# A hybrid decoder layer on one core: the last adaLN split is read wholly in the down projection, and the sums of the tokens' quadrants run on VectorE over more steps

## The chip, the cores and the metric

The kernel runs on one core of one Trainium2 chip. The metric is the device time of one launch in microseconds (us). Engines are named as in the profile: PE is TensorE, DVE is VectorE, ACT is ScalarE, POOL is GpSimd, SP is SyncE, which here only issues DMAs. Each engine takes its own instructions in the order in which they were written.

## The reference, cut to what matters

One decoder layer over 512 tokens of width 2048, all in float32:

```python
mod = jax.nn.silu(c) @ w_ada[l] + b_ada[l]
sh_a, sc_a, gt_a, sh_f, sc_f, gt_f = [m[:, None, :] for m in jnp.split(mod, 6, axis=-1)]
h = rmsnorm(x, g_pre_attn[l]) * (1.0 + sc_a) + sh_a
proj = h @ w_in[l]                     # q, k, v of 8 dilated and 8 differential heads
...
x = x + gt_a * rmsnorm(mix @ w_out[l], g_post_attn[l])
h = rmsnorm(x, g_pre_ffn[l]) * (1.0 + sc_f) + sh_f
f = (jax.nn.silu(h @ w_gate[l]) * (h @ w_up[l])) @ w_down[l]      # D_FF = 5632
x = x + gt_f * rmsnorm(f, g_post_ffn[l])
```

`w_ada` has six splits of 2048x2048, 16 MB each. The last of them gives `gt_f`, which is used only on the output of the down projection.

## The kernel before

**Steps.** All weights pass through one list of 544 steps. A step takes one weight tile of 128x1024 (512 KB), splits it into a high and a low part and multiplies three times (high by high, low by high, high by low), which gives float32 accuracy. The names in the profile: `w_raw` is the tile as it was loaded, `w_hi` its high part (a copy on ACT, L1530), `w_lo` the rest (a subtraction on DVE, L1539); the matmuls stand on L282 to L284. The list has these stages:

- steps 0 to 79: input projections, with attention mixed in;
- W0 + 0 to 63 (W0 = step 80): output projection, 12 matmuls a step. The tokens are done in two halves: the first half's result comes at W0 + 32, and from there its residual, norm (`u`, `x`, `wss`; L1132 to L1156) and transposes into the FFN's input (`h2_tr`, L1178 to L1196) run beside the second half;
- F0 + 0 to 31 (F0 = step 144): gate and up columns of the first of 11 column groups, 12 matmuls a step. In F0 + 0 to 15 the second half's residual, norm and transposes run;
- F1 + 0 to 279 (F1 = step 176): the other ten groups in a Strassen-like form with seven products. Four of these read sums of the tokens' quadrants, the tiles `e`;
- D0 + 0 to 87 (D0 = step 456): down projection, 24 matmuls a step, four column groups of 22 steps.

**Look-ahead.** In step i the kernel makes `w_hi` and `w_lo` of step i + 2 (`do_hi`, `do_lo`). There are three buffers each for `w_hi` and `w_lo`, and a ring of four buffers for `w_raw`; SP issues the next load when a buffer has been used (`pump_loads`).

**adaLN reads.** Four of the six splits (array `in_adar`, 32 tiles of 512 KB each) are read through the same ring of four, as extra items behind a step (`aux[i]`). DVE turns each tile into one column by a multiply with a running sum (L228; `ada_dot`). A planner decides ahead of the run behind which steps they go, with an estimate of when DVE and the DMAs have room. The order is split n = 2, 0, 1, 3; what is left of n = 3 after the output projection goes behind steps D0 + 2 and on. When all of n = 3 is there, three small DVE operations, a transpose on PE and two DMAs through DRAM (`ada_row`) make the row `gtg` of gains, which `d_evac` multiplies to the down projection's result.

**Quadrant sums.** For each of eight chunks j: `e_load` reads the chunk from DRAM (SP), `e_sums` makes four sums of 128x256 on POOL (L1233 to L1236), and `e_split` makes the high part `e` on ACT (L1247) and the low part on DVE (L1248). They stand at F0 + 16 + 2j, + 17 + 2j and + 19 + 2j. The buffers for them are the tiles `stage` and `stageb`.

The order in one step, from the loop that issues all (the quoted lines are not adjacent):

```python
for f in start_ev[i]: f()
s["mm"](*hl[i], 0)                     # first half of the matmuls
do_hi(i + LA)                          # ACT: w_hi of step i + 2
s["mm"](*hl.pop(i), 1)
for f in post_ev[i]: f()
do_lo(i + LA)                          # DVE: w_lo of step i + 2, SP: next loads
for j, (src, f) in enumerate(aux[i]): ...   # DVE: adaLN products, SP: next loads
for f in post_end[i]: f()
```

Of the kernel before, what the change touches and what calls it, by code (L numbers as in the profile page):

```python
# [24 lines left out]
M_ADA = -0.05  # L25
# [9 lines left out]
def body(tc, t):  # L35
# [5 lines left out]
    with ctx:  # L41
# [986 lines left out]
        for i, c in dve_late.items():  # L1028
            dve_cost[i] += c
        todo = [(hn, k, h, qbs) for hn, (k, h) in enumerate(order)  # L1030
                for qbs in (((0,), (1,), (2,), (3,)) if k == "B" else ((0, 1), (2,), (3,)))]
        ada_todo = [(n, ch, hf) for n in (2, 0, 1, 3) for ch in range(16) for hf in range(2)]
        need = defaultdict(int)
# [17 lines left out]
        for i in range(W0 + 60):  # L1051
# [23 lines left out]
            t_dma = max(t_dma, t_pe) + 1.45 * (1 + len(aux[i]))  # L1075
            while ada_todo and (ada_todo[0][0] == 3 or i < W0 + 46) and i >= 1 and t_dve + 1.14 <= t_end + (M_ADA if i < W0 else M_ADAW) and \
                    t_dma + 1.45 <= t_end + M_DMA and len(aux[i]) < NAUX:
                t_dma += 1.45
                n, ch, hf = ada_todo.pop(0)
                aux[i].append((adar[n, ch, hf], ada_use(n, ch, hf)))  # L1080
                t_dve += 1.14
                aux_last = (i, i - W0, n, ch)
                if n < 2:
                    if ch == 15 and hf:
                        post_end[i].append(lambda n=n: ada_cols(n))
                elif n == 2 and ch == 15 and hf:
# [9 lines left out]
        assert not todo and not rq and not rows_todo, (len(todo), len(rq))  # L1096
        assert len(ada_todo) <= 16 and all(a[0] == 3 for a in ada_todo), ada_todo


        start_ev[W0 + 62].append(lambda: [act.dma_start(silud[:, 1024 * h:1024 * h + 1024], silu_h[h]) for h in range(2)])  # L1100

# [5 lines left out]
        for i, (n, ch, hf) in enumerate(ada_todo):  # L1107
            aux[D0 + 2 + i].append((adar[n, ch, hf], ada_use(n, ch, hf)))
        row = ada_row(3, 7)
        post_late[D0 + 18].append(row[0])  # L1110
        mid_ev[D0 + 19].insert(0, row[1])
        start_ev[D0 + 20].append(row[2])

# [104 lines left out]
        def v3(p, a):  # L1218
            return p[1].rearrange("p (a c) -> p a c", a=a)
# [10 lines left out]
        def e_sums(j):  # L1230
            h, e = v3(esum[j], 4), stage.get()
            o = v3(e, 4)
            pool.tensor_tensor(o[:, 0, :], h[:, 2, :], h[:, 3, :], op=OP.subtract)  # L1233
            pool.tensor_tensor(o[:, 1, :], o[:, 0, :], h[:, 0, :], op=OP.subtract)
            pool.tensor_tensor(o[:, 2, :], h[:, 0, :], h[:, 2, :], op=OP.subtract)
            pool.tensor_tensor(o[:, 3, :], h[:, 1, :], o[:, 1, :], op=OP.add)  # L1236
            stage.add(esum[j])
            esum[j] = e

        def e_split(j):  # L1240
            if ("E", 0, 0) not in SA:
                for lo, tags in enumerate((LR[4:], ("P2", "P5", "P0", "P3"))):
                    for m in range(4):
                        SA["E", lo, m] = U(tags[m], [128, 2, 4, 256], R, name=f"e{lo}{m}")
            o = v3(esum[j], 4)
            hi, lo = SA["E", 0, j // 2][:, j % 2], SA["E", 1, j // 2][:, j % 2]
            act.activation(hi, o, AF.Copy)  # L1247
            dve.tensor_tensor(lo, o, hi.bitcast(F), op=OP.subtract)  # L1248
            stage.add(esum.pop(j))
# [71 lines left out]
        def stage_alloc(n):  # L1321
# [275 lines left out]
        for i in range(NSTEP):  # L1597
# [158 lines left out]
```

## Time and profile before

| | us |
|---|---|
| median of 3 runs | 2279.52 |
| lowest and highest run | 2278.01, 2283.3 |
| the profiled execution, its own time | 2278.92 |
| its span in the trace | 2277.1 |
| PE busy in the span | 2222.8 (98%) |
| DVE busy | 1594.9 (70%) |
| ACT busy | 1032.8 (45%) |
| POOL busy | 74.2 (3%) |

The share of busy time says that PE sets the time; the 54 us in which it is idle are few, so they have to be looked for stage by stage. A matmul's end is modelled: each is shown 0.39 us long while the next starts 0.23 us later, so idle time of PE is a little more than the gaps that the trace prints.

### The profile page before, as it was taken

The page shows a single profiled execution, that of the slowest core. Times are in us where ns is not written, and L with a number is a line of the kernel's source. Part 1 is how long each engine was busy: PE and PEld are TensorE (multiplying, and loading weights), DVE is VectorE, ACT ScalarE, POOL GpSimd, SP SyncE. Part 2 cuts the span into 40 slices and gives each one's busy share as a digit, 9 for nine tenths or more (in the row PEclk, how much of TensorE's full clock was granted, in tenths as well). Part 3 has the DMA queues.
Part 4 walks back from the last instruction along what each step waited for, and adds up shares of the span by engine and source line. Part 5 has one row for each costly group of instructions (what it writes and reads, how often), then busy time and mean ns, then how long its engine had stood idle before and what let it go on. Part 6 is the DMA issues. An engine that isn't in the chain of part 4 may idle for free.

```text
span 2277.1 us, 26712 instructions
## 1 busy us (share of the span) xinstructions
PE 2222.8 (98%) x10012; PEld 1808.3 (79%) x10012; DVE 1594.9 (70%) x2201; ACT 1032.8 (45%) x1507; POOL 74.2 (3%) x68
## 2 busy tenths in 40 slices
PE   7999999999999888999999999999999999999998
PEld 6888777778887666778888888888888888888886
DVE  6987877776777786777778777777777644444445
ACT  5443344444435454644454444444444433333432
POOL 0000000000001000150000000000000000000000
PEclk8999999999999999999999999999999999999999
DMA  9796544456778888864224323422432656655564
GB/s 370 296 332 213 157 139 166 145 163 192 222 260 278 300 295 300 276 240 147 94 93 157 130 98 115 157 93 93 157 140 80 252 194 211 195 189 200 189 218 185
DMA packets 124802, 440.11 MB, mean 193 GB/s; under 512 B 13792, under 2 KB 25344, under 8 KB 118272
## 3 DMA queue, kind: packets, MB, share of 16 engines
q1 hardware_dynamic: 105936, 406.14, 51.8%
q10 hardware_dynamic: 18736, 32.27, 4.4%
q8 instruction: 78, 1.28, 0.2%
q14 instruction: 52, 0.43, 0.1%
HBM read 404.25 MB, written 25.18 MB: 189 GB/s over the span
## 4 chain that ended last, share of the span: by engine, by line
PE 83%; DMA 6%; DVE 6%; issue 2%; ACT 2%; POOL 1%; ACTq 0%; SPq 0%; DVEq 0%; POOLq 0%
PE b L283 21%; PE b L284 21%; PE b L282 20%; PE b L277 5%; PE b L279 5%; PE b L278 5%; DMA w_raw<-in_wout 5%; DVE w_lo L1539 2%; PE b L507 2%; PE b L545 1%; ACT w_hi L1530 1%; DVE w_raw L228 1%; PE b L1262 1%; PE b L500 1%; PE b L529 1%
## 5 line engine op out<-in xcount | busy, mean ns | idle before, releaser
L1539 DVE TENSOR_TENSOR w_lo<-w_raw,w_hi 128x1024 fp32r<-128x1024 f32 x264 | 325.6, 1237 | 312.9 <-ACT w_hi L1530 312.5
L1530 ACT ACTIVATE w_hi<-w_raw 128x1024 fp32r<-128x1024 f32 x264 | 278.7, 1057 | 461.6 <-PE b L284 309.2
L283 PE MATMUL b<-w_lo,h 128*128 128x512 f32 x864 | 338.6, 392 | 7.7 <-DVE w_lo L1539 6.2
L282 PE MATMUL b<-w_hi,h 128*128 128x512 f32 x864 | 342.1, 396 | 0.4 <-ACT xT L212 0.4
L284 PE MATMUL b<-w_hi,h 128*128 128x512 f32 x864 | 337.1, 390 | 0.0
L1530 ACT ACTIVATE w_hi<-raw 128x1024 fp32r<-128x1024 f32 x196 | 208.1, 1062 | 268.9 <-PE b L284 244.3
L1539 DVE TENSOR_TENSOR w_lo<-raw,w_hi 128x1024 fp32r<-128x1024 f32 x196 | 240.1, 1229 | 103.1 <-ACT w_hi L1530 102.6
L284 PE MATMUL b<-w_hi,acthl 128*128 128x512 f32 x704 | 274.0, 389 | 0.4 <-DVE acthl L972 0.4
L282 PE MATMUL b<-w_hi,acthl 128*128 128x512 f32 x704 | 274.1, 389 | 0.0
L283 PE MATMUL b<-w_lo,acthl 128*128 128x512 f32 x704 | 273.9, 389 | 0.0
L282 PE MATMUL b<-w_hi,e 128*128 128x512 f32 x640 | 249.7, 390 | 0.0
L283 PE MATMUL b<-w_lo,e 128*128 128x512 f32 x640 | 249.0, 389 | 0.0
L284 PE MATMUL b<-w_hi,e 128*128 128x512 f32 x640 | 249.0, 389 | 0.0
L277 PE MATMUL b<-h,w_hi 128*128 128x512 f32 x512 | 213.4, 417 | 0.0
L278 PE MATMUL b<-h,w_hi 128*128 128x512 f32 x512 | 201.0, 393 | 1.6 <-DVE h L273 1.6
L279 PE MATMUL b<-h,w_lo 128*128 128x512 f32 x512 | 201.6, 394 | 0.0
L283 PEld LDWEIGHTS b<-w_lo,h 128*128 128x128 f32 x864 | 162.3, 188 | 48.1 <-DVE w_lo L1539 15.0
L282 PEld LDWEIGHTS b<-w_hi,h 128*128 128x128 f32 x864 | 162.2, 188 | 37.5 <-issue 3.7
L284 PEld LDWEIGHTS b<-w_hi,h 128*128 128x128 f32 x864 | 162.2, 188 | 33.6
L284 PEld LDWEIGHTS b<-w_hi,acthl 128*128 128x128 f32 x704 | 132.1, 188 | 28.0 <-DVE acthl L972 0.8
L282 PEld LDWEIGHTS b<-w_hi,acthl 128*128 128x128 f32 x704 | 132.1, 188 | 27.8 <-DVE stage L1314 0.2
L283 PEld LDWEIGHTS b<-w_lo,acthl 128*128 128x128 f32 x704 | 132.2, 188 | 27.3
(246 smaller groups left out, 3262.8 us busy)
## 6 DMA issues: line engine op xcount, KB each, us to landing
w_raw<-in_adar SPq DMA_DIRECT2D x128, 512.0 KB, 4.6
raw<-in_wgu SPq DMA_DIRECT2D x109, 512.0 KB, 4.5
w_raw<-in_win SPq DMA_DIRECT2D x107, 512.0 KB, 5.0
actf<-act2d SPq DMA_DIRECT2D x88, 512.0 KB, 4.7
w_raw<-in_wdown SPq DMA_DIRECT2D x88, 512.0 KB, 3.5
w_raw<-in_wout SPq DMA_DIRECT2D x64, 512.0 KB, 4.9
w_lent<-in_wgu SPq DMA_DIRECT2D x51, 512.0 KB, 4.6
ada<-in_ada SPq DMA_DIRECT2D x21, 1024.0 KB, 9.2
```

The costliest lines, as they stand in the source:

```text
L228: dve.scalar_tensor_tensor(w, w, 1.0, silu_h[half], op0=OP.mult, op1=OP.mult, accum_out=dst)
L277: pe.matmul(ps, whi, ahi, start=start, stop=False, **kw)
L278: pe.matmul(ps, whi, alo, start=False, stop=False, **kw)
L279: pe.matmul(ps, wlo, ahi, start=False, stop=stop, **kw)
L282: pe.matmul(ps, ahi, whi, start=start, stop=False, **kw)
L283: pe.matmul(ps, ahi, wlo, start=False, stop=False, **kw)
L284: pe.matmul(ps, alo, whi, start=False, stop=stop, **kw)
L500: pe.matmul(sc[:, r], qk[:, i, qs], qk[:, i + 1, :N], start=True, stop=True)
L507: pe.matmul(sc[:, :N], qk[k, 2 * m, qs], qk[k, 2 * m + 1, :N], start=True, stop=True)
L529: pe.transpose(tr[:, j, :], misc["p"][:, n % 2, 128 * j:128 * j + 128], ident)
L1530: act.activation(hi, raw, AF.Copy)
L1539: dve.tensor_tensor(lo, raw, hi.bitcast(F), op=OP.subtract)
```

## The change

Three things, and small ones that go with them:

1. The planner places the splits n = 2, 0, 1 only. All 32 tiles of n = 3 go behind D0 + 2 to D0 + 33, one a step. The row of gains then comes at D0 + 36 and no longer at D0 + 20, which is after the first column group's evacuation (D0 + 22, 23). So that group is copied out bare, and its gain is multiplied on later (`d_gain`, at D0 + 46, 48, 50, 52). The transpose uses PSUM bank 3 in place of 7. The copy of silu(c) to DRAM, which the late reads need, is issued at W0 + 50 in place of W0 + 62.
2. The quadrant sums run on DVE. They stand at the end of step F0 + 17 + floor(5j/2), the copy on ACT with them, the low part one step later, the load three steps earlier.
3. The transposes of the FFN's input come one step later, in both halves.

```diff
-        ada_todo = [(n, ch, hf) for n in (2, 0, 1, 3) for ch in range(16) for hf in range(2)]
+        ada_todo = [(n, ch, hf) for n in (2, 0, 1) for ch in range(16) for hf in range(2)]
...
-            while ada_todo and (ada_todo[0][0] == 3 or i < W0 + 46) and i >= 1 and t_dve + 1.14 <= t_end + (M_ADA if i < W0 else M_ADAW) and \
+            while ada_todo and i < W0 + 46 and i >= 1 and t_dve + 1.14 <= t_end + (M_ADA if i < W0 else M_ADAW) and \
...
+        ada_todo = [(3, ch, hf) for ch in range(16) for hf in range(2)]
...
-        start_ev[W0 + 62].append(lambda: [act.dma_start(silud[:, 1024 * h:1024 * h + 1024], silu_h[h]) for h in range(2)])
+        start_ev[W0 + 50].append(lambda: [act.dma_start(silud[:, 1024 * h:1024 * h + 1024], silu_h[h]) for h in range(2)])
...
-        row = ada_row(3, 7)
-        post_late[D0 + 18].append(row[0])
-        mid_ev[D0 + 19].insert(0, row[1])
-        start_ev[D0 + 20].append(row[2])
+        row = ada_row(3, 3)
+        post_late[D0 + 34].append(row[0])
+        mid_ev[D0 + 35].insert(0, row[1])
+        start_ev[D0 + 36].append(row[2])
...
-            pool.tensor_tensor(o[:, 0, :], h[:, 2, :], h[:, 3, :], op=OP.subtract)
-            pool.tensor_tensor(o[:, 1, :], o[:, 0, :], h[:, 0, :], op=OP.subtract)
-            pool.tensor_tensor(o[:, 2, :], h[:, 0, :], h[:, 2, :], op=OP.subtract)
-            pool.tensor_tensor(o[:, 3, :], h[:, 1, :], o[:, 1, :], op=OP.add)
+            dve.tensor_tensor(o[:, 0, :], h[:, 2, :], h[:, 3, :], op=OP.subtract)
+            dve.tensor_tensor(o[:, 1, :], o[:, 0, :], h[:, 0, :], op=OP.subtract)
+            dve.tensor_tensor(o[:, 2, :], h[:, 0, :], h[:, 2, :], op=OP.subtract)
+            dve.tensor_tensor(o[:, 3, :], h[:, 1, :], o[:, 1, :], op=OP.add)
...
+            act.activation(SA["E", 0, j // 2][:, j % 2], o, AF.Copy)
+        def e_lo(j):
...
-        post_ev[F0 + 8].append(lambda: stage_alloc(0))
+        post_ev[F0 + 2].append(lambda: stage_alloc(0))
...
-            post_ev[F0 + 16 + 2 * j].append(lambda j=j: e_load(j))
-            post_ev[F0 + 17 + 2 * j].append(lambda j=j: e_sums(j))
-            post_ev[F0 + 19 + 2 * j].append(lambda j=j: e_split(j))
+            at = F0 + 17 + 5 * j // 2
+            start_ev[at - 3].append(lambda j=j: e_load(j))
+            post_end[at].append(lambda j=j: e_sums(j))
+            post_end[at + 1].append(lambda j=j: e_lo(j))
...
-            pe_ev[b1 + 8 + i].append((0, a))
-            post_ev[b1 + 8 + i].append(b)
+            pe_ev[b1 + 9 + i].append((0, a))
+            post_ev[b1 + 9 + i].append(b)
...
-            pe_ev[b1 + 7 + i].append((0, a))
-            post_ev[b1 + 7 + i].append(b)
+            pe_ev[b1 + 8 + i].append((0, a))
+            post_ev[b1 + 8 + i].append(b)
...
-            dve.tensor_tensor(u, ps, GTG[1][:, cg, :], op=OP.mult)
+            if cg == 0:
+                dve.tensor_copy(u, ps)
+            else:
+                dve.tensor_tensor(u, ps, GTG[1][:, cg, :], op=OP.mult)
...
+            if i - D0 in (46, 48, 50, 52):
+                d_gain((i - D0 - 46) // 2)
```

**The loads on SP in the output projection.** In the kernel before, around the load of the tokens `x` for the first half (W0 + 20), an adaLN tile stands behind nearly every second weight tile:

```order
L1515 DMA w_raw<-in_adar 128x1024
L1515 DMA w_raw<-in_wout 128x1024 x2
L1128 DMA x_5898<-in_xtok 128x2048
L1128 DMA x_5900<-in_xtok 128x2048
L1515 DMA w_raw<-in_adar 128x1024
L1515 DMA w_raw<-in_wout 128x1024
L1515 DMA w_raw<-in_adar 128x1024
L1515 DMA w_raw<-in_wout 128x1024 x2
```

In the changed kernel, from the last adaLN tile of the stage to its last weight tile:

```order
L1523 DMA w_raw<-in_adar 128x1024
L1523 DMA w_raw<-in_wout 128x1024 x9
L1129 DMA x_5889<-in_xtok 128x2048
L1129 DMA x_5891<-in_xtok 128x2048
L1523 DMA w_raw<-in_wout 128x1024 x32
L1129 DMA x_6642<-in_xtok 128x2048
L1129 DMA x_6644<-in_xtok 128x2048
L1523 DMA w_raw<-in_wout 128x1024 x6
```

From W0 + 16 on the ring now holds weight tiles alone: 30 adaLN tiles, 15.7 MB, have left this stage for D0 + 2 to D0 + 33.

**DVE and ACT in the second half of the first group (F0 + 17 on).** DVE before, for two chunks; the operation on `e` is the low part of a chunk:

```order
L1539 TENSOR_TENSOR w_lo<-w_raw,w_hi 128x1024 x2
L1248 TENSOR_TENSOR e_7473<-stage_7161,e_7469 128x1024
L1539 TENSOR_TENSOR w_lo<-w_raw,w_hi 128x1024 x2
L1248 TENSOR_TENSOR e_7474<-stage_7392,e_7470 128x1024
L1539 TENSOR_TENSOR w_lo<-w_raw,w_hi 128x1024 x2
```

DVE in the changed kernel, for one chunk and the next one's start:

```order
L1547 TENSOR_TENSOR w_lo<-w_raw,w_hi 128x1024
L1234 TENSOR_TENSOR stage_7304<-stageb 128x256
L1235 TENSOR_TENSOR stage_7304<-stage_7304,stageb 128x256
L1236 TENSOR_TENSOR stage_7304<-stageb 128x256
L1237 TENSOR_TENSOR stage_7304<-stageb,stage_7304 128x256
L1547 TENSOR_TENSOR w_lo<-w_raw,w_hi 128x1024
L1247 TENSOR_TENSOR e_7337<-stage_7304,e_7333 128x1024
L1547 TENSOR_TENSOR w_lo<-w_raw,w_hi 128x1024 x2
L1234 TENSOR_TENSOR stage_6928<-stage_7304 128x256
```

ACT in the changed kernel, around the chunks j = 2 and 3 and the gate of the second half:

```order
L1538 ACTIVATE w_hi<-w_raw 128x1024 x3
L1244 ACTIVATE e_7334<-stage_6928 128x1024
L1538 ACTIVATE w_hi<-w_raw 128x1024 x2
L1244 ACTIVATE e_7334<-stage_7304 128x1024
L1538 ACTIVATE w_hi<-w_raw 128x1024
L1279 ACTIVATE stage_7304<-b_7288 128x512
L1279 ACTIVATE stage_7304<-b_7297 128x512
L1538 ACTIVATE w_hi<-w_raw 128x1024 x2
```

The four sums are now DVE's own, and between them and DVE's next `w_lo` two copies stand on ACT: the chunk's `e`, then the `w_hi` that this `w_lo` reads.

## Rows read from the trace of the kernel before

**Rows 1.** The profile page: busy time by engine, and PE's busy share, in tenths, in 40 slices of 57 us.

```profile
PE 2222.8 (98%) x10012; PEld 1808.3 (79%) x10012; DVE 1594.9 (70%) x2201; ACT 1032.8 (45%) x1507; POOL 74.2 (3%) x68
...
PE   7999999999999888999999999999999999999998
```

**Rows 2.** Busy time by stretch: from and to, length, busy time of PE, PEld, DVE, ACT and POOL (instructions), granted clock, DMA share, GB/s. In order: a stretch of the input projections, W0 + 16 to 63, F0 + 0 to 14, F0 + 15 to F1 + 2, the rest of F1, the first steps of the down projection, a later stretch of it.

```profile
114.00:171.00 57.00, 57.00 (x253) 47.18 (x253) 50.98 (x86) 25.75 (x33) 0.00 (x0) 1.00 0.91 331
...
734.80:903.70 168.90, 146.36 (x609) 113.61 (x608) 124.38 (x175) 77.52 (x117) 3.69 (x4) 0.96 0.86 306
903.70:949.20 45.50, 45.40 (x214) 36.72 (x213) 37.68 (x55) 34.48 (x54) 4.65 (x4) 1.00 0.77 257
949.20:1013.00 63.80, 57.58 (x257) 46.17 (x256) 43.96 (x35) 31.00 (x32) 37.71 (x32) 1.00 0.76 285
1013.00:1784.00 771.00, 769.77 (x3459) 636.09 (x3458) 588.49 (x533) 371.73 (x423) 0.00 (x0) 1.00 0.35 120
1788.00:1804.00 16.00, 16.00 (x77) 13.24 (x76) 11.59 (x12) 8.60 (x12) 0.00 (x0) 1.00 0.99 351
1810.00:1980.00 170.00, 170.00 (x752) 140.65 (x751) 76.12 (x71) 65.17 (x72) 0.00 (x0) 1.00 0.61 204
```

**Rows 3.** Instructions in order of time on PE and, last, the chain of work: the first matmuls of the steps F0 + 0 and F0 + 1 (start, us), then the transposes of two steps that have them (start, us, four of 128x128).

```profile
903.70 0.39 PE L282 MATMUL b<-w_hi,h 128*128 128x512 f32 x1
...
906.42 0.39 PE L282 MATMUL b<-w_hi,h 128*128 128x512 f32 x1
...
926.83 0.44 PE b L1178 x4
930.04 0.44 PE b L1178 x4
```

**Rows 4.** What PE waited for from 734.8 to 903.7 us: us in total, times, the longest.

```profile
PE b L283 <- DVE w_lo L1539: 12.7, 15, 2.5
PE b L282 <- ACT w_hi L1530: 4.5, 3, 3.8
PE b L1178 <- DVE x L1156: 3.7, 1, 3.7
PE b L283 <- DVE wss L1145: 1.5, 1, 1.5
```

**Rows 5.** The same stretch: what the copy `w_hi` waited for (one group on ACT, with its idle time and what ended it), the DMA issues (count, KB each, median us to landing), and the adaLN products on DVE.

```profile
L1530 ACT ACTIVATE w_hi<-w_raw 128x1024 fp32r<-128x1024 f32 x49 | 51.9, 1059 | 85.0 <-DMA w_raw<-in_wout 69.3 <-DVE w_raw L228 6.9 <-PE b L284 5.5
...
L228 DVE SCALAR_TENSOR_TENSOR w_raw<-w_raw,silu_b 128x1024 f32<-128x1024 f32 x16 | 19.5, 1219 | 0.7 <-DMA w_raw<-in_adar 0.7
...
w_raw<-in_wout SPq DMA_DIRECT2D x45, 512.0 KB, 4.9
w_raw<-in_adar SPq DMA_DIRECT2D x29, 512.0 KB, 4.5
x<-in_xtok SPq DMA_DIRECT2D x4, 1024.0 KB, 8.4
```

**Rows 6.** The same stretch: the clock in the three pieces where it was lower, and the chain's step through the slowest weight load (start, us).

```profile
751.10:754.50 3.40, 3.40 (x10) 2.64 (x8) 2.49 (x5) 1.67 (x3) 0.00 (x0) 0.51 0.84 318
819.50:822.80 3.30, 3.10 (x9) 2.61 (x10) 2.59 (x6) 2.41 (x5) 0.00 (x0) 0.50 0.80 245
877.50:884.20 6.70, 4.87 (x11) 3.51 (x12) 5.17 (x6) 3.17 (x3) 0.00 (x0) 0.50 0.86 299
...
867.42 10.22 DMA w_raw<-in_wout
```

**Rows 7.** PE's largest idle time from 949.2 to 1013 us, and what PE waited for in that stretch as a whole.

```profile
994.20 0.50 PE L283 MATMUL b<-w_lo,h 128*128 128x512 f32 x1 [1.93 <-DVE w_lo L1539]
...
PE b L283 <- DVE w_lo L1539: 6.2, 5, 1.9
```

**Rows 8.** ACT and DVE there in order of time: start, us, and in brackets idle time and what ended it.

```profile
957.51 1.06 ACT L1530 ACTIVATE w_hi<-w_raw 128x1024 fp32r<-128x1024 f32 x1 [1.66 <-PE b L284]
...
976.00 1.06 ACT L1247 ACTIVATE e<-stage 128x1024 fp32r<-128x1024 f32 x1 [1.50 <-POOL stage L1236]
976.97 1.04 ACT L1530 ACTIVATE w_hi<-w_raw 128x1024 fp32r<-128x1024 f32 x1
...
990.16 1.06 ACT L1247 ACTIVATE e<-stage 128x1024 fp32r<-128x1024 f32 x1 [3.46 <-POOL stage L1236]
...
958.61 1.23 DVE L1539 TENSOR_TENSOR w_lo<-w_raw,w_hi 128x1024 fp32r<-128x1024 f32 x1 [1.49 <-ACT w_hi L1530]
```

**Rows 9.** Groups by line and shape from 734.8 to 1013 us: the 128x256 operation of two SBUF operands on DVE, one of POOL's sums, products out of PSUM on DVE, and the gate's copy out of PSUM on ACT.

```profile
L1195 DVE TENSOR_TENSOR h<-h2t,h 128x256 fp32r<-128x256 f32 x32 | 13.5, 420 | 2.4 <-ACT h L1194 2.0
...
L1235 POOL TENSOR_TENSOR stage<-stageb 128x256 f32<-128x256 f32 x3 | 5.2, 1718 | 0.0
...
L1281 DVE TENSOR_TENSOR stage<-stage,b 128x512 f32<-128x512 f32 x4 | 2.6, 678 | 1.8 <-ACT stage L1280 1.8
...
L1280 ACT ACTIVATE stage<-b 128x512 f32<-128x512 f32 x4 | 2.2, 592 | 0.0
```

**Rows 10.** DVE in step D0 + 2, the first of the down projection that has an adaLN tile (start, us).

```profile
1800.28 1.23 DVE L1539 TENSOR_TENSOR w_lo<-w_raw,w_hi 128x1024 fp32r<-128x1024 f32 x1 [3.08 <-ACT w_hi L1530]
1801.42 1.22 DVE L972 TENSOR_TENSOR acthl<-actf,acthl 128x1024 fp32r<-128x1024 f32 x1
1802.56 1.22 DVE L228 SCALAR_TENSOR_TENSOR w_raw<-w_raw,silu_back 128x1024 f32<-128x1024 f32 x1
```

More of the change, by code (lines that the diff above doesn't have):

```diff
@@ L1096, in body @@
         assert not todo and not rq and not rows_todo, (len(todo), len(rq))
-        assert len(ada_todo) <= 16 and all(a[0] == 3 for a in ada_todo), ada_todo
-        start_ev[W0 + 62].append(lambda: [act.dma_start(silud[:, 1024 * h:1024 * h + 1024], silu_h[h]) for h in range(2)])
+        assert not ada_todo
+        ada_todo = [(3, ch, hf) for ch in range(16) for hf in range(2)]
+        start_ev[W0 + 50].append(lambda: [act.dma_start(silud[:, 1024 * h:1024 * h + 1024], silu_h[h]) for h in range(2)])
         def silu_back():
@@ L1232, in e_sums @@
             o = v3(e, 4)
-            pool.tensor_tensor(o[:, 0, :], h[:, 2, :], h[:, 3, :], op=OP.subtract)
-            pool.tensor_tensor(o[:, 1, :], o[:, 0, :], h[:, 0, :], op=OP.subtract)
-            pool.tensor_tensor(o[:, 2, :], h[:, 0, :], h[:, 2, :], op=OP.subtract)
-            pool.tensor_tensor(o[:, 3, :], h[:, 1, :], o[:, 1, :], op=OP.add)
+            dve.tensor_tensor(o[:, 0, :], h[:, 2, :], h[:, 3, :], op=OP.subtract)
+            dve.tensor_tensor(o[:, 1, :], o[:, 0, :], h[:, 0, :], op=OP.subtract)
+            dve.tensor_tensor(o[:, 2, :], h[:, 0, :], h[:, 2, :], op=OP.subtract)
+            dve.tensor_tensor(o[:, 3, :], h[:, 1, :], o[:, 1, :], op=OP.add)
             stage.add(esum[j])
             esum[j] = e
-        def e_split(j):
             if ("E", 0, 0) not in SA:
@@ L1244, in e_split @@
                         SA["E", lo, m] = U(tags[m], [128, 2, 4, 256], R, name=f"e{lo}{m}")
-            o = v3(esum[j], 4)
+            act.activation(SA["E", 0, j // 2][:, j % 2], o, AF.Copy)
+        def e_lo(j):
             hi, lo = SA["E", 0, j // 2][:, j % 2], SA["E", 1, j // 2][:, j % 2]
-            act.activation(hi, o, AF.Copy)
-            dve.tensor_tensor(lo, o, hi.bitcast(F), op=OP.subtract)
+            dve.tensor_tensor(lo, v3(esum[j], 4), hi.bitcast(F), op=OP.subtract)
             stage.add(esum.pop(j))
@@ L1476, in d_evac, with d_gain @@
             act.activation(u, ps, AF.Square, accum_out=HF["dss", tb][:, cg:cg + 1])
-            dve.tensor_tensor(u, ps, GTG[1][:, cg, :], op=OP.mult)
+            if cg == 0:
+                dve.tensor_copy(u, ps)
+            else:
+                dve.tensor_tensor(u, ps, GTG[1][:, cg, :], op=OP.mult)
+        def d_gain(tb):
+            u = HF["du", tb][:, 0, :]
+            dve.tensor_tensor(u, u, GTG[1][:, 0, :], op=OP.mult)
         def d_out(tb, c0, n):
```

## The prediction, made before the changed kernel ran

> **What bounds the kernel now.** I read the busy times first, then the slices [rows 1]: PE is busy 2222.8 of 2277.1 us, and the slices show where the other 54 us lie: the first slice (filling, not touched), slices 14 to 16, and the last (draining, not touched). So a gain has to come from around slices 14 to 16: the output projection, and perhaps the first FFN group behind it. The stretches [rows 2] cut these by step. A step without extra work is 12 matmuls; two steps start at 903.70 and 906.42, 2.72 us apart, 0.227 us a matmul, and a step with four transposes takes 3.21, 0.49 more [rows 3].
>
> - W0 + 16 to 63: 48 steps and eight sets of transposes should take 48 x 2.72 + 8 x 0.49 = 134.5 us. They took 168.9: **34.4 too many**.
> - F0 + 0 to 14: 15 x 2.72 + 8 x 0.49 = 44.7; they took 45.5: 0.8 too many.
> - F0 + 15 to F1 + 2: 20 steps and 16 transposes, 54.4 + 2.0 = 56.4; they took 63.8: **7.4 too many**.
> - The rest of F1 and the down projection: PE idle 1.2 us in 771, and none in 170 [rows 2].
>
> In the first stretch PE waits for `w_lo`, for `w_hi`, and once 3.7 us for the norm `x` that the transposes read [rows 4]. Behind the first two stands the load: ACT idled 85.0 us there before `w_hi`, 69.3 of it until an `in_wout` tile landed [rows 5]. Its three long stalls also cost clock: the granted clock is half (1.2 in place of 2.4 GHz) for 3.4, 3.3 and 6.7 us [rows 6], which loses half of 13.4, 6.7 us, part of the 34.4.
>
> Why the load is late: a ring buffer goes round in 4.9 us of landing, 1.06 of `w_hi`, 1.23 of `w_lo` [rows 5, 8], some 7.2 us. Four buffers give an item each 1.8 us. The stretch has 30 adaLN tiles on 48 weight tiles, 1.62 items a step: 2.9 us, more than the 2.72 that PE needs. That is a stall in the mean, before the token loads `x` (landing 8.4) or one weight tile that took 10.22 [rows 5, 6].
>
> **The change part by part.** The sum is made against the profiled execution, 2278.9 us; the median of the runs is 0.6 above it.
>
> *1. The adaLN tiles leave W0 + 16 to 63.* With one item a step the ring gives a weight tile each 1.8 us against 2.72. Only when a landing takes over 4 x 2.72 - 2.3 = 8.6 us can it stall; the 10.22 behind the token loads did. Each of the two token loads delays a few tiles by at most 10.22 - 8.6 = 1.6. DVE also loses 30 products of 1.22 [rows 5]. The nearest row for what is left is F0 + 0 to 14, which does the same residual, norm and transposes with weight loads alone and moves 257 GB/s: 0.8 us in 15 steps [rows 2]. For 48 steps I take 2 us (bounds 1 and 6: the second if both token loads cost their 1.6 and the norm again about 2). The transposes come one step later, 2.72 us more for the one wait of 3.7 [rows 4]; it is inside this term. Term: **-34.4 + 2 = -32.4**.
>
> *2. The same tiles in D0 + 2 to 33.* A step of 24 matmuls is 5.44 us and now takes three tiles of 0.524 MB, 289 GB/s. Two stretches show PE without idle time at more: 331 GB/s for 57 us and 351 for 16 [rows 2]. The ring has two items a step, 2 x 1.8 = 3.6 of 5.44 us. DVE has 76.1 of 170 us busy there [rows 2], 45%; a product of 1.14 a step makes it 66%, behind `w_lo` and `acthl` as in step D0 + 2 [rows 10]. The row of gains is due at D0 + 44 and is loaded at D0 + 36. Four gains of some 0.7 [rows 9] lie in the same spare time. If that cover were gone, 32 x 1.14 + 4 x 0.7 = 39 us would lie open. Term: **0** (bounds 0 and 3).
>
> *3. The quadrant sums.* Before: ACT's `e` waits for POOL's last sum, 3.46 us in one case, with the next `w_hi` queued behind it [rows 8]; POOL's sum of 128x256 takes up to 1.72 us [rows 9], and PE stalls five times, 1.9 us at most [rows 7]. That wait goes. What is late next: on DVE, in order, `w_lo`, four sums, then the next `w_lo`, which needs a `w_hi` that stands on ACT behind `e`, and `e` needs the sums. So from the last sum to the next `w_lo` DVE has nothing: 0.97 for `e` (976.00 to 976.97 [rows 8]) and 1.06 for `w_hi`, 2.0 us for each of eight chunks, where before POOL's time ran beside DVE. DVE's time from F0 + 17 to F0 + 35:
>
> - 19 `w_lo`, 8 low parts of `e`, 4 sums of weights, 31 x 1.14 (pace of neighbours, 1801.42 to 1802.56 [rows 10]) = 35.3;
> - 32 sums of 128x256. Alone one lasts 0.42 [rows 9]; neighbours overlap by 0.08 [rows 10]: 0.34 to 0.42 each, 10.9 to 13.4;
> - 6 products out of PSUM x 0.68 [rows 9] = 4.1;
> - 8 holes x 2.0, less 1.3 that two of these products fill, plus 0.6 for a gate copy [rows 9] that stands in one = 15.3.
>
> Together 65.6 to 68.1 us. PE's 19 steps and 16 transposes take 51.7 + 2.0 = 53.7: a lack of 11.9 to 14.4. `w_lo` runs ahead at the start: the one that began at 958.61 ended some 2.5 us into its step (ACT's copy for it began at 957.51, with the step) [rows 8], and is due at 2 x 2.72 + 0.23 = 5.7, so the lead is 3.2. So PE should stall 8.7 to 11.2 in sum; I take 10 for the 7.4 of before, +2.6. One stall should come near 3 us (chunk 3's sums, then the second half's gate, all before one `w_lo`); the halved clock followed stalls of 2.5 us and more, and none followed 1.93 [rows 4, 6, 7]. One such piece loses 1.7. Term: **+4.3** (bounds -2.4, if only half the holes open, and +7.5, with two lowered pieces).
>
> The Trainium skill says of successive VectorE operations that the next does not start until the pipe has emptied (VectorE: DVE Perf Modes, "The DRAIN you can't avoid"). The starts 1.14 us apart of operations that last 1.22 [rows 10] speak against it. By the rule the sums would be the 13.4, by the rows alone 10.9; dependent neighbours may lie between.
>
> Sum: 2278.9 - 32.4 + 0 + 4.3 = 2250.8; with the 0.6 to the median, **2251 us**. Bounds of the terms together: 2244 to 2262.
>
> **The rivals.**
>
> *The sums run free on DVE.* If the holes are covered by the lead each time (the chunks are 2.5 steps apart, not two, which favours it), the second half of the group runs like its first: 0.8 in place of 7.4. Time: 2279.5 - 32.4 - 6.6 = 2240. For it: DVE is busy only 44 of 63.8 us there [rows 2]. Against it: `w_lo` already idles on `w_hi`, 1.49 us in one case [rows 8], so idle DVE time cannot be used. The Trainium skill's table for choosing an engine gives elementwise work to VectorE, two-input operations on GpSimd being about twice as slow (GPSIMD Engine Reference, "Engine selection"). By that the group would only gain.
>
> *The long stalls stay.* If the three that cost clock come from the token loads and the norm rather than from the adaLN tiles, they stay: 2.5 + 3.7 + 3.8 idle and 6.7 of clock, 16.7 in place of 2. Time: 2251 + 15 = 2266. For it: the slowest tile was issued right behind the token loads [rows 6]. Against it: it would have had 8.6 us, and F0 + 0 to 14 has the same norm without a stall.
>
> *The down projection starves, slower than before.* There the ring has two items a step, so it stalls when landings last beyond 2 x 5.44 - 2.3 = 8.6 us for all 32 steps. At 10.2, as behind the token loads, each step lacks 0.8 us, 26 in all, and nearly the whole gain is gone; above 10.3 the kernel gets slower, at 11 by 32 x 1.2 = 38 - 28 = 10: 2290. For it: the stretch that stalls now moves 306 GB/s, near the 289. Against it: 331 and 351 without idle PE, and landings of 4.5 to 4.9 even in the stretch that moves 306 [rows 2, 5].
>
> That the reads do not move is ruled out by the order of the loads.
>
> **How the numbers follow.** Forecast 0.64 (2244 to 2262), sums free 0.13 (2240), long stalls stay 0.16 (2266), starving 0.04, something that leaves no difference 0.03. The range 2240 to 2263 holds the forecast, most of the first rival and part of the second. A measurement of this kernel can tell about 0.2%, 4.6 us: faster 0.93, within it 0.03, slower 0.04.
>
> **What would show it.** In the changed profile W0 + 16 to 63 should take 135 to 141 us at full clock with no wait for a load over 2 us. In the first group's second half PE should wait for `w_lo` in the steps after a chunk's sums, DVE idle before `w_lo` until `w_hi`, ACT having done `e` just before; some 8.7 to 11 us too many. D0 + 2 to 33 should take 32 x 5.44 us at about 290 GB/s. Wrong would be: idle PE in the down projection; a load that still ends PE's waits in the output projection; no wait behind the sums.

## The result, and the profile after

| | before | changed |
|---|---|---|
| median, us | 2278.77 (4 runs) | 2248.38 (4 runs) |
| lowest and highest | 2276.07, 2283.3 | 2246.85, 2249.17 |
| the profiled execution, its own time | 2278.92 | 2247.79 |

The ratio is 0.9864, 95% interval 0.9847 to 0.9881: 30.4 us faster. 2251 was forecast.

The stretches of the changed kernel that answer to [rows 2], with the same columns: W0 + 16 to 63, F0 + 0 to 14, F0 + 15 to 34, F0 + 35 to 38 and a little, the rest of F1, D0 + 2 to 33, a later stretch of the down projection.

```profile
732.70:868.20 135.50, 135.06 (x610) 110.97 (x609) 89.33 (x115) 77.47 (x117) 3.69 (x4) 1.00 0.78 266
868.20:913.50 45.30, 45.24 (x212) 36.48 (x211) 36.72 (x52) 33.30 (x52) 4.65 (x4) 1.00 0.75 246
913.50:974.40 60.90, 57.44 (x259) 46.54 (x258) 45.65 (x64) 29.96 (x34) 0.00 (x0) 1.00 0.81 301
974.40:992.20 17.80, 14.95 (x51) 10.95 (x50) 15.70 (x18) 7.20 (x10) 0.00 (x0) 0.81 0.09 29
992.20:1752.00 759.80, 758.58 (x3409) 626.90 (x3408) 576.54 (x522) 365.38 (x415) 0.00 (x0) 1.00 0.35 121
1767.00:1942.00 175.00, 175.00 (x778) 145.05 (x777) 114.75 (x134) 67.75 (x74) 0.00 (x0) 1.00 0.86 293
1950.00:2100.00 150.00, 150.00 (x663) 124.08 (x662) 69.94 (x64) 56.88 (x63) 0.00 (x0) 1.00 0.59 200
```

The first row is the gain: 135.5 us in place of 168.9, full clock, PE idle for 0.4. The third and the fourth hold what the change costs, the fourth most of all: four steps that should take 11 to 12 us take 17.8, at a mean clock of 0.81. The sixth shows the down projection carrying 293 GB/s with no idle PE.

From the first matmul of one step to that of another, in both traces:

| stretch | before | changed | difference |
|---|---|---|---|
| start to W0 + 16 | 734.8 | 732.7 | -2.1 |
| W0 + 16 to 63 | 168.9 | 135.5 | -33.4 |
| F0 + 0 to 14 | 45.5 | 45.4 | -0.1 |
| F0 + 15 to 38 | 74.9 | 78.7 | +3.8 |
| F0 + 39 to the end | 1253.0 | 1253.8 | +0.8 |

The first row is not an effect of the change, whose instructions there are the same: in the other kernels below, with the same instructions up to W0 + 15, that stretch of the output projection takes 57.3 to 58.9 us from one trace to the next (58.0 before, 56.5 in this one).

What PE waited for in the changed kernel, as in [rows 4], from 732.7 to 868.2 us:

```profile
PE b L283 <- DVE w_lo L1547: 0.4, 1, 0.4
```

And what ended ACT's idle time before `w_hi` there, as in [rows 5]:

```profile
L1538 ACT ACTIVATE w_hi<-w_raw 128x1024 fp32r<-128x1024 f32 x49 | 51.9, 1060 | 55.3 <-PE b L284 40.3 <-DMA w_raw<-in_wout 5.9 <-issue 4.0
```

ACT now waits for PE, 40.3 us, to free a buffer; for a load it waits 5.9 us in place of 69.3. The stage has changed its bound from the loads to PE.

The loads themselves did not get faster. In the same stretch (count, KB each, median us to landing):

```profile
w_raw<-in_wout SPq DMA_DIRECT2D x44, 512.0 KB, 4.9
```

The median is the 4.9 us of before [rows 5], and the slowest took 10.35 us where 10.22 was the slowest before. What changed is the number of items that go round the ring of four in a step.

The four sums and what stands behind them, in order of time, DVE and then ACT (start, us; in brackets idle time and what ended it), chunk 3 of the changed kernel:

```profile
942.63 1.22 DVE L1547 TENSOR_TENSOR w_lo<-w_raw,w_hi 128x1024 fp32r<-128x1024 f32 x1
943.77 0.42 DVE L1234 TENSOR_TENSOR stage<-stage 128x256 f32<-128x256 f32 x1
944.22 0.42 DVE L1235 TENSOR_TENSOR stage<-stage,stage 128x256 f32<-128x256 f32 x1
944.57 0.42 DVE L1236 TENSOR_TENSOR stage<-stage 128x256 f32<-128x256 f32 x1
944.90 0.42 DVE L1237 TENSOR_TENSOR stage<-stage,stage 128x256 f32<-128x256 f32 x1
947.87 1.28 DVE L1280 TENSOR_TENSOR stage<-stage,b 128x512 f32<-128x512 f32 x2 [2.55 <-ACT stage L1279]
949.07 1.22 DVE L1547 TENSOR_TENSOR w_lo<-w_raw,w_hi 128x1024 fp32r<-128x1024 f32 x1
```

```profile
945.35 1.06 ACT L1244 ACTIVATE e<-stage 128x1024 fp32r<-128x1024 f32 x1 [4.07 <-DVE stage L1237]
946.32 1.04 ACT L1538 ACTIVATE w_hi<-w_raw 128x1024 fp32r<-128x1024 f32 x1
947.26 1.06 ACT L1279 ACTIVATE stage<-b 128x512 f32<-128x512 f32 x2
```

This is the hole of the prediction. The sums end at 945.32. ACT has stood idle 4.07 us in front of `e`; then come `e`, `w_hi` and the gate. DVE does nothing for 2.55 us, and the `w_lo` that was due ends at 950.29. The matmul that reads it started at 950.35, after 2.44 us of idle PE:

```profile
950.35 0.50 PE L283 MATMUL b<-w_lo,h 128*128 128x512 f32 x1 [2.44 <-DVE w_lo L1547]
```

Behind the sums of six of the other seven chunks DVE stood idle for 2.07 or 2.08 us until `w_hi` was there. Here is chunk 7:

```profile
982.86 1.22 DVE L1547 TENSOR_TENSOR w_lo<-raw,w_hi 128x1024 fp32r<-128x1024 f32 x1 [2.07 <-ACT w_hi L1538]
```

Only behind chunk 6's did two products out of PSUM fill most of the hole; 0.88 us was left.

### The profile page after: what moved, and what is told of

It reads as the page before. It is cut to its first block, busy times and chain, and to the rows that moved or that the text cites. A ratio compares the mean times of both kernels' runs of the same rounds, so it can differ in the third digit from the quotient of the medians.

```text
span 2246.0 us, 26703 instructions
## 1 busy us (share of the span) xinstructions
PE 2213.5 (99%) x10012; PEld 1806.3 (80%) x10012; DVE 1601.2 (71%) x2237; ACT 1031.7 (46%) x1507; POOL 36.5 (2%) x36
## 4 chain that ended last, share of the span: by engine, by line
PE 91%; DVE 4%; DMA 2%; ACT 1%; issue 1%; POOL 0%; SPq 0%; DVEq 0%; POOLq 0%; ACTq 0%
PE b L283 24%; PE b L284 23%; PE b L282 23%; PE b L277 5%; PE b L279 5%; PE b L278 5%; PE b L507 2%; DVE w_lo L1547 1%; PE b L545 1%; DMA w_raw<-in_wout 1%; PE b L1261 1%; PE b L529 1%; PE b L500 1%; ACT w_hi L1538 1%; DVE w_raw L228 1%
```

## The experiments

All are edits of the changed kernel unless said otherwise. The ratios are to runs of the kernel before on the same chip: with a median of 2278.55 us for *ada_only*, *sums_only*, *copy_behind* and *half_back*, 2279.03 for *reads_alone*, *products_alone*, *two_a_step* and *pool_spread*, 2279.32 for *away* and *tr_early*. Their times:

| run | median, us | ratio to before, 95% interval | W0 + 16 to 63, us | F0 + 15 to 38, us |
|---|---|---|---|---|
| before | 2278.77 | | 168.9 | 74.9 |
| changed | 2248.38 | 0.9864, 0.9847 to 0.9881 | 135.5 | 78.7 |
| ada_only | 2245.29 | 0.9853, 0.9838 to 0.9869 | 135.8 | 75.5 |
| sums_only | 2281.36 | 1.0013, 1.0004 to 1.0023 | 167.6 | 78.6 |
| copy_behind | 2238.84 | 0.9824, 0.9807 to 0.9841 | 134.8 | 68.1 |
| pool_spread | 2239.60 | 0.9825, 0.9808 to 0.9841 | 135.4 | 69.3 |
| reads_alone | 2282.41 | 1.0015, 1.0005 to 1.0025 | 171.2 | 77.1 |
| products_alone | 2254.68 | 0.9893, 0.9879 to 0.9908 | 142.1 | 77.6 |
| half_back | 2258.93 | 0.9910, 0.9893 to 0.9928 | 146.0 | 78.7 |
| away | 2254.07 | 0.9888, 0.9873 to 0.9903 | 142.4 | 77.6 |
| two_a_step | 2248.32 | 0.9863, 0.9848 to 0.9877 | 135.3 | 76.6 |
| tr_early | 2250.28 | 0.9874, 0.9857 to 0.9890 | 136.8 | 77.6 |

### The two large parts, each alone

*ada_only* keeps the sums on POOL with the spacing, the copy and the low part as before:

```diff
-            dve.tensor_tensor(o[:, 0, :], h[:, 2, :], h[:, 3, :], op=OP.subtract)
...
+            pool.tensor_tensor(o[:, 0, :], h[:, 2, :], h[:, 3, :], op=OP.subtract)
...
-            post_end[at].append(lambda j=j: e_sums(j))
+            post_ev[F0 + 17 + 2 * j].append(lambda j=j: e_sums(j))
+            post_ev[F0 + 19 + 2 * j].append(lambda j=j: e_split(j))
```

> Part 1 and the later transposes as changed; the quadrant sums stay on POOL as before. Theory (the ring caused the output projection's stalls; the sums on DVE open holes before w_lo): W0 + 16 to 63 takes 135 to 137 us, F0 + 15 on has the 7 to 8 us too many of before and not the 11.5 of the changed kernel, time 2244 to 2247 us, some 3 faster than the changed kernel. Rival (the sums on DVE are a gain of their own): slower than the changed kernel, 2250 to 2256 us.

Measured: 2245.3 us, 3.1 less than the changed kernel, the output projection at 135.8, the group at 75.5. The move of the reads is the whole gain, and the other part costs. By themselves the 3.1 us are close to the scatter (one of the four runs took 2248.5); *sums_only* finds the cost again.

*sums_only* is the kernel before with `e_sums`, `e_lo` and their places as in the changed one.

> The kernel before with the quadrant sums on DVE over more steps, and nothing else. Theory: F0 + 15 to F1 + 6 has 11 us too many in place of 7.5, time 2281 to 2285 us (before: 2278.8). Rival (sums on DVE are a gain): 2271 to 2276 us.

Measured: 2281.4 us, the interval of the ratio just above one. F0 + 15 to 38 takes 78.6 us as in the changed kernel, and 74.9 before. The two parts add up: against the 2278.55 of before beside them they are -33.3 and +2.8, together -30.5; -30.4 was measured for both.

### Is it the hole behind the sums, or DVE's work?

*copy_behind* moves one ACT instruction behind the next `w_hi`:

```diff
-            act.activation(SA["E", 0, j // 2][:, j % 2], o, AF.Copy)
...
+        def e_hi(j):
+            act.activation(SA["E", 0, j // 2][:, j % 2], v3(esum[j], 4), AF.Copy)
...
+            post_ev[at + 1].append(lambda j=j: e_hi(j))
```

> The changed kernel with one thing moved: ACT makes a chunk's e one step later, behind the next w_hi, so that DVE's next w_lo no longer waits for it. Theory (holes): without the 8 x 2 us of holes DVE's 50 to 53 us fit into PE's 53.7, and the stalls from F0 + 15 to F1 + 6 fall from 11.5 to 0 to 3 us; 2237 to 2241 us. Rival (DVE has too much work there, wherever e stands): 8 us or more stay, 2245 to 2249 us.

Measured: 2238.8 us, 9.5 less than the changed kernel. DVE does the same work. Its rows for chunk 3 and its neighbours, DVE of *copy_behind*:

```profile
941.91 0.42 DVE L1234 TENSOR_TENSOR stage<-stage 128x256 f32<-128x256 f32 x1
...
943.04 0.42 DVE L1237 TENSOR_TENSOR stage<-stage,stage 128x256 f32<-128x256 f32 x1
943.97 1.29 DVE L1282 TENSOR_TENSOR stage<-stage,b 128x512 f32<-128x512 f32 x2 [0.52 <-ACT stage L1281]
945.17 1.22 DVE L1550 TENSOR_TENSOR w_lo<-w_raw,w_hi 128x1024 fp32r<-128x1024 f32 x1
```

and the stretch F0 + 15 to 38 as a whole (columns as above):

```profile
913.90:982.00 68.10, 67.71 (x308) 55.68 (x306) 59.93 (x79) 38.53 (x43) 0.00 (x0) 1.00 0.75 278
```

The idle time behind the sums is 0.52 us in place of 2.55, and PE is idle 0.4 us in 68.1 with DVE busy for 59.9. DVE had the room; the order took it away.

*pool_spread* puts the sums on POOL again, and `e` three steps later and behind that step's `w_hi`:

```diff
-            dve.tensor_tensor(o[:, 0, :], h[:, 2, :], h[:, 3, :], op=OP.subtract)
...
+            pool.tensor_tensor(o[:, 0, :], h[:, 2, :], h[:, 3, :], op=OP.subtract)
...
+            start_ev[at].append(lambda j=j: e_sums(j))
+            post_ev[at + 3].append(lambda j=j: e_hi(j))
+            post_end[at + 3].append(lambda j=j: e_lo(j))
```

> The changed kernel with the sums on POOL again, at the changed spacing of 2.5 steps, begun one step earlier in the order, and a chunk's e and its low part two to three steps behind the sums, behind that step's w_hi. Theory (what stalls is w_hi queued behind an e that waits; which engine sums matters little): 0 to 3 us too many from F0 + 15 to F1 + 6, 2237 to 2242 us, as with the sums on DVE and the copy moved. Rival (POOL's sums cost by themselves, 1.7 us each beside DVE): 2245 to 2250 us.

Measured: 2239.6 us, level with *copy_behind*, although POOL's sums take as long as before (groups on POOL in F0 + 15 to 38):

```profile
L1236 POOL TENSOR_TENSOR stageb<-stage 128x256 f32<-128x256 f32 x3 | 5.2, 1717 | 0.0
```

So the engine of the sums is worth little. What is worth 9 us is that nobody's `w_hi` stands behind a copy that has to wait. *copy_behind* shows this by one moved instruction; *pool_spread* agrees with it, but against *ada_only* it has the wider spacing as well.

While POOL makes sums, POOL and DVE slow each other down. DVE and then POOL of *pool_spread*:

```profile
943.76 3.44 DVE L1550 TENSOR_TENSOR w_lo<-w_raw,w_hi 128x1024 fp32r<-128x1024 f32 x2
...
930.60 0.73 POOL L1236 TENSOR_TENSOR stage<-stageb 128x256 f32<-128x256 f32 x1
944.40 1.73 POOL L1236 TENSOR_TENSOR stage<-stage 128x256 f32<-128x256 f32 x1
```

Two `w_lo` take 3.44 us here; elsewhere one takes 1.22 and the next starts 1.14 later. A sum on POOL takes 0.72 to 0.75 us where DVE does nothing, as at 930.60, and in most cases 1.6 to 1.8 beside DVE's operations. The kernel before has the same, with some 1.75 us for a `w_lo` beside POOL's sums. The prediction left this out: moving the sums also gives DVE's other operations back their pace. With the order right it is worth little, since *pool_spread* takes only 2.0 us more than the 67.3 that PE needs there.

### What of the adaLN tiles made the stalls: the reads or the products?

*reads_alone* reads the 30 tiles at their old steps and leaves the products out (a copy of one column in their place; in the down projection too, so the row of gains lacks them):

```diff
+        for i in range(W0 + 16, W0 + 60):
+            if (i - W0) % 3:
+                n, ch, hf = ada_todo.pop(0)
+                aux[i].append((adar[n, ch, hf], read_only(n, ch, hf)))
```

> The changed kernel with the 30 adaLN tiles read again in W0 + 16 to 59, at the steps they had before; their products are left out (a copy of one column each), also in the down projection, so the row of gains lacks them. Theory (ring: the reads make the stalls): most of the 33.5 us comes back, W0 + 16 to 63 takes 155 to 168, time 2268 to 2281 us. Rival (DVE's products made them): 135 to 139, 2248 to 2252 us.

*products_alone* gives DVE 30 operations of that size and reads nothing:

```diff
+        for i in range(W0 + 16, W0 + 60):
+            if (i - W0) % 3:
+                post_end[i].append(lambda k=i % 2: dve.reduce_sum(junk[:, 0:1], silu_h[k], axis=mybir.AxisListType.X))
```

> The changed kernel with 30 more DVE operations in W0 + 16 to 59, each a sum over 128x1024 elements of a tile that is there already, as long as an adaLN product; nothing more is read. Theory (ring): W0 + 16 to 63 takes 135 to 139 us, time 2248 to 2252. Rival (DVE): 155 to 168, 2268 to 2281 us.

Measured: 171.2 us for the reads alone, 142.1 for the products alone. The first stretch below is *reads_alone*:

```profile
733.60:904.90 171.30, 148.64 (x610) 115.64 (x609) 92.82 (x145) 77.38 (x117) 2.84 (x4) 0.95 0.85 302
```

and this is *products_alone*:

```profile
734.40:876.50 142.10, 137.64 (x609) 110.45 (x608) 122.02 (x145) 77.30 (x117) 3.69 (x4) 1.00 0.76 255
```

DVE is busy 92.8 us in the first and 122.0 in the second, and the first is the slow one. What ACT waited for before `w_hi`, *reads_alone* and then *products_alone*:

```profile
L1546 ACT ACTIVATE w_hi<-w_raw 128x1024 fp32r<-128x1024 f32 x49 | 51.9, 1058 | 89.5 <-DMA w_raw<-in_wout 81.7 <-PE b L1187 3.9 <-DVE red L1110 1.9
...
L1541 ACT ACTIVATE w_hi<-w_raw 128x1024 fp32r<-128x1024 f32 x49 | 51.8, 1060 | 52.3 <-PE b L284 34.1 <-DMA w_raw<-in_wout 11.7 <-issue 4.4
```

The reads bring back the whole of it, 2 us more than before even. (The one-column copy that is left makes DVE wait 7.5 us for landings, little beside the 81.7.) The products are not free as the theory had it (135 to 139 was expected): they cost 6.6 us when they stand alone, and add nothing where the reads already stall.

### How much of them does the stage carry?

*half_back* returns 15 tiles, one behind every third step from W0 + 16:

```diff
+        for k in range(15):
+            n, ch, hf = ada_todo.pop(0)
+            aux[W0 + 16 + 3 * k].append((adar[n, ch, hf], ada_use(n, ch, hf)))
```

> The changed kernel with 15 of the 30 adaLN tiles back in the output projection, one behind every third step from W0 + 16 on, the other 17 from D0 + 2 on. Theory (ring: a stall begins only when items per step x 1.8 us pass 2.72): 1.31 items a step x 1.8 = 2.4 us, under 2.72, so W0 + 16 to 63 takes 136 to 140 us and the whole 2249 to 2253 us. Rival (each tile costs its share, 34 us / 30): 15 x 1.1 = 17 us, 2265 us.

Measured: 146.0 us, 10.5 more than the changed kernel, between the two theories. The steps that took over 0.3 us too long were W0 + 19, 22, 24, 25, 38 to 40, 52 and 57. Three stretches of *half_back*: W0 + 19 to 27, the ten steps behind them, and W0 + 52 and 53:

```profile
745.00:772.00 27.00, 24.52 (x103) 19.02 (x103) 19.10 (x28) 12.95 (x22) 0.00 (x0) 1.00 0.85 314
772.00:799.00 27.00, 27.00 (x120) 22.14 (x119) 21.80 (x29) 14.34 (x24) 1.74 (x2) 1.00 0.80 268
...
845.00:856.00 11.00, 8.52 (x31) 6.96 (x32) 7.45 (x9) 4.79 (x6) 0.00 (x0) 0.84 0.78 285
```

With the same one tile in three steps, PE idles 2.5 us around the first token load (issued at 751.24, landed at 761.28) and not at all behind it. So the mean of the ring was not the whole.

The third stretch, 4.3 of the 10.5 us, is not the second token load's. PE's wait in it, that load's issue, and the two halves of the copy of silu(c) to DRAM (issue, then us to landing of each):

```profile
847.48 0.79 PE L283 MATMUL b<-w_lo,mixhi 128*128 128x512 f32 x1 [2.53 <-DVE w_lo L1550]
...
849.01 0.86 SPq L1132 DMA_DIRECT2D x<-in_xtok  x2
...
837.13 0.33 ACTq L1101 DMA_DIRECT2D silud<-p  x1
837.50 0.53 ACTq L1101 DMA_DIRECT2D silud<-silu_b  x1
...
silud<-p ACTq DMA_DIRECT2D x1, 512.0 KB, 8.3
silud<-silu_b ACTq DMA_DIRECT2D x1, 512.0 KB, 10.4
```

The wait ended 1.5 us before the token load was issued. In flight during it was the copy of silu(c), 837.13 to 847.89, which the change itself moved to W0 + 50. In the changed kernel the same copy runs without an adaLN tile beside it, and W0 + 49 to 53 are not slow. That the two together made the stall is read from their times; no run took the copy away.

*away* tests that, with 12 tiles kept off the token loads and the norm:

```diff
+        for k in (26, 28, 30, 32, 34, 41, 43, 45, 47, 49, 58, 60):
+            n, ch, hf = ada_todo.pop(0)
+            aux[W0 + k].append((adar[n, ch, hf], ada_use(n, ch, hf)))
```

> The changed kernel with 12 adaLN tiles back in the output projection, at the steps W0 + 26 to 34, 41 to 49 (every second) and 58 and 60: away from the token loads (W0 + 20 and 52) and from the norm (W0 + 36 to 40). Theory, after the 15 tiles in every third step cost 10.5 us mostly in W0 + 19 to 25, 37 to 40 and 52: the ring alone carries 1.5 items a step x 1.8 = 2.7 us, and a stall needs a token load or the norm's DVE work beside it; W0 + 16 to 63 takes 135 to 138 us, time 2248 to 2251. Rival (each tile costs its share, 10.5 / 15 = 0.7 us, wherever it stands): 8 us, W0 + 16 to 63 144 us, time 2257.

Measured: 142.4 us and 2254.1, again between, nearer to the rival. Stretches of *away*: W0 + 16 to 18, ahead of all its tiles; W0 + 19 to 34, with five tiles, one at every second step from W0 + 26; W0 + 50 to 53:

```profile
734.60:745.00 10.40, 8.66 (x36) 6.33 (x35) 6.74 (x12) 6.69 (x13) 0.00 (x0) 1.00 0.67 238
745.00:790.00 45.00, 44.97 (x199) 36.92 (x198) 32.81 (x50) 23.48 (x40) 0.41 (x1) 1.00 0.82 285
...
835.00:850.00 15.00, 13.17 (x55) 10.27 (x56) 11.56 (x15) 8.04 (x15) 0.00 (x0) 1.00 0.90 337
```

Of the 6.9 us over the changed kernel, some 2.5 lie ahead of its first tile, in W0 + 17 and 18 at 3.9 us each (*ada_only* and *tr_early* also took 3.9 for W0 + 17), so they are not the tiles'. At 1.5 items a step the ring carried W0 + 26 to 34 with no stall. The rest came in the norm's steps, 1.8 us, and in W0 + 48 to 53, 3.2 us, nearly all of it ahead of the second token load (issued at 846.99) and again with the copy of silu(c) in flight (835.61 to 844.51). In the norm's steps *products_alone* loses 3.3 us without a read, so there it can be DVE's products. That every tile costs its share wherever it stands is refuted; what one costs beside other traffic is not settled by these two runs.

### Does the down projection have room?

*two_a_step* puts two tiles behind each of D0 + 2 to 17:

```diff
-            aux[D0 + 2 + i].append((adar[n, ch, hf], ada_use(n, ch, hf)))
+            aux[D0 + 2 + i // 2].append((adar[n, ch, hf], ada_use(n, ch, hf)))
```

> The changed kernel with two adaLN tiles a step at D0 + 2 to 17 in place of one a step at D0 + 2 to 33. Four tiles of 0.524 MB in 5.44 us are 385 GB/s, three items a step in the ring. Theory (a stage starves when items per step x round trip / 4 passes its step; 3 x 1.8 = 5.4 is the edge, at a landing of 7 us it is 7.0): D0 to D0 + 33 takes 8 to 25 us more than 186, time 2256 to 2273 us. Rival (the down projection has room for more yet): 2247 to 2250 us.

Measured: 2248.3 us, as the changed kernel. The sixteen steps, of *two_a_step*:

```profile
1767.00:1854.20 87.20, 87.20 (x388) 72.22 (x387) 68.45 (x87) 30.68 (x32) 0.00 (x0) 1.00 0.97 350
```

PE is never idle in 87.2 us at 350 GB/s. The expectation was wrong: it put the edge at landings of 5 us and a loss at 7, and the loads landed in 5.5 us (adaLN) and 5.8 (weights) in the median. Its round trip of 7.2 us also counts a `w_hi` copy that an adaLN tile doesn't have. Starving was further off than the prediction priced it.

### The later transposes

*tr_early* undoes the shift of the first half's transposes:

```diff
-            pe_ev[b1 + 9 + i].append((0, a))
-            post_ev[b1 + 9 + i].append(b)
+            pe_ev[b1 + 8 + i].append((0, a))
+            post_ev[b1 + 8 + i].append(b)
```

> The changed kernel with the first half's transposes one step earlier, at W0 + 40 to 47 as before. Theory (the wait of 3.7 us for the norm was DVE late behind adaLN products, so without these the later step is not needed): 0 to 1.5 us more in W0 + 38 to 41, time 2248 to 2250 us. Rival (the norm itself is late, and the later step is what removed the wait): 3 us or more of it back, 1.7 of clock with it, 2252 to 2254 us.

Measured: 2250.3 us, 1.9 more than the changed kernel; the intervals overlap. The transposes' wait is back with 0.76 us of the 3.71:

```profile
802.55 0.55 PE L1179 MATMUL b<-cst,x 128*128 128x128 f32 x3 [0.76 <-DVE x L1157]
```

The step with it, W0 + 39, takes 4.06 us. So the wait of before was mostly DVE late behind the adaLN tiles (reads or products, not told apart here); the later step is worth about a microsecond.

## Why the prediction was right, point by point

- **The output projection: -32.4 forecast, -33.4 measured.** The place and the bound hold: PE waited for loads that the adaLN reads held up (*reads_alone*, 171.2 us). The model behind it, a ring with a mean rate of an item per 1.8 us, is too coarse: with 1.31 items a step it gave no stall, and *half_back* lost 10.5 us around the first token load, the norm and the copy of silu(c). Past its edge of 8.6 us for a single landing little happened: three loads of the changed kernel took longer, and PE waited 0.4 us in all. The remainder of 2 us was 1.0. DVE's products, which the prediction counted inside this term, are worth 6.6 us by themselves and nothing on top of the reads.
- **The down projection: 0 forecast, 0.1 us measured** for D0 to D0 + 33 (186.14 before, 186.26 changed), at 293 GB/s where 289 was worked out. DVE is busy 114.75 of 175 us, 66% as forecast.
- **The quadrant sums: +4.3 forecast, +3.8 measured.** The 10 us of stalls plus 1.7 of clock make 11.7 too many; F0 + 15 to 38 should take 24 x 2.72 + 2.0 = 67.3 and took 78.7, 11.4 too many. The holes of the eight chunks were 15.9 us in sum, 15.3 worked out; the rows of chunk 3 and *copy_behind* show that they are the cause. *two_a_step* has the same instructions in this stretch, kept the full clock and took 76.6: 9.3 us of stalls, inside 8.7 to 11.2, which leaves 2.1 for the lowered clock of this trace. Its place was wrong: it was forecast for the stall behind chunk 3, which came (2.44 us) without it, and it came at F0 + 37. That the profiled execution had one such loss is luck; by the trace the same stretch takes 76.6 to 78.7 us, which is +1.7 to +3.8. The bounds of this term do not follow from the numbers beside them: half the holes less, 7.6 us, leave 1.1 to 3.6 of stalls, so -6.3 to -3.8 in place of -2.4, and 11.2 with two lowered pieces gives +7.2 in place of +7.5.
- **The pace of the sums.** Four of them took 1.55 us from 943.77 to 945.32, 0.33 to 0.45 from start to start: between the two prices, and the longest step is the one to an operation that reads the one before it. Where one does not depend, the next starts 0.07 to 0.09 us before the end of the one ahead. The Trainium skill's section that the prediction cites (VectorE: DVE Perf Modes, "The DRAIN you can't avoid") adds that a next operation which is not held starts earlier; the rows agree with that addition, and the prediction left it out.
- **The sums run free on DVE (0.13): no.** By the Trainium skill's table (GPSIMD Engine Reference, "Engine selection") VectorE was the place for them, GpSimd being about twice as slow, and as a duration that holds here (0.42 us against 0.74 on an undisturbed POOL and up to 1.8 beside DVE); as a time of the kernel it does not: *ada_only* is faster by 3.1 us, and the engine is level once the order is right (*pool_spread*).
- **The long stalls stay (0.16): no.** No wait of PE in the stretch is over 0.4 us. Their part in the truth is that other traffic decides where a ring that also carries adaLN tiles stalls (*half_back*). Their price was a little high: in the 13.4 us at half clock PE was busy for 11.4 [rows 6], so at most 5.7 us were lost there and not 6.7.
- **Starving (0.04): no**, and not even at 350 GB/s.

The best versions here are *copy_behind* and, level with it, *pool_spread*, faster than both kernels: 2238.8 us for the first, ratio to before 0.9824 (0.9807 to 0.9841).

## What to carry to other kernels

Put optional reads in the stage whose loads PE does not wait for, and find it by what ends the wait of the engine that first touches the loaded tile, not by PE's busy share. Before moving work to another engine, follow the in-order queue of the engine behind it: an instruction that waits delays all that stands behind it, and moving that one copy behind the next step's copy was worth 9.5 us, three times the 3.1 that moving the sums had cost. Price a full ring where it meets other large transfers, since its mean rate shows no stall there; list all of them by their times of issue and landing, also those that the change itself moves.

## What was not expected of the hardware

The prediction took from the trace before that the clock halves (1.2 in place of 2.4 GHz) after stalls of 2.5 us and more. In the changed kernel it did not fall after 2.44 us of idle PE (at 950.35), and it fell for 6.8 us after one of 1.84 with shorter ones about it:

```profile
978.25 0.50 PE L283 MATMUL b<-w_lo,e 128*128 128x512 f32 x1 [0.38 <-DVE w_lo L1547]
982.88 0.63 PE L282 MATMUL b<-w_hi,e 128*128 128x512 f32 x1 [1.84 <-ACT w_hi L1538]
984.14 0.80 PE L283 MATMUL b<-w_lo,e 128*128 128x512 f32 x1 [0.63 <-DVE w_lo L1547]
...
983.10:989.90 6.80, 6.17 (x15) 4.56 (x15) 6.80 (x7) 4.45 (x7) 0.00 (x0) 0.50 0.23 77
```

The same stalls, of 0.39, 1.83 and 0.77 us, came at the same steps in *two_a_step*, with no lower clock there:

```profile
979.07 0.50 PE L283 MATMUL b<-w_lo,e 128*128 128x512 f32 x1 [0.39 <-DVE w_lo L1547]
983.71 0.49 PE L282 MATMUL b<-w_hi,e 128*128 128x512 f32 x1 [1.83 <-ACT w_hi L1538]
984.97 0.50 PE L283 MATMUL b<-w_lo,e 128*128 128x512 f32 x1 [0.77 <-DVE w_lo L1547]
...
978.00:992.00 14.00, 10.62 (x44) 7.58 (x43) 11.90 (x14) 7.29 (x10) 0.00 (x0) 1.00 0.11 37
```

In *away* a stall of 2.44 us at the same step as the changed kernel's was followed by 3.4 us at half clock:

```profile
959.24 0.50 PE L283 MATMUL b<-w_lo,h 128*128 128x512 f32 x1 [2.44 <-DVE w_lo L1550]
...
959.90:963.30 3.40, 3.40 (x10) 2.64 (x9) 3.37 (x5) 0.00 (x0) 0.00 (x0) 0.50 0.83 294
```

So of stalls of about 2 us the length alone does not tell whether the clock falls. For F0 + 15 to 38, with the same instructions, it made some 2 us between traces: 76.6 us without a lowered piece (*two_a_step*), 77.6 with two of 3.4 us (*away*), 78.7 with one of 6.8 (the changed kernel). What decides it was not tried.
